# Stream work over sparse attention: value jobs of two head pairs opened a pair earlier, even shares, three score buffers

## The chip, the cores and the metric

The kernel runs on one core of a Trainium2 chip. A core has TensorE (PE; PEld is its weight load), VectorE (DVE), ScalarE (ACT), GpSimd (POOL) and SyncE (SP, which issues most DMAs). The metric is the device time of one execution in microseconds; the figure of a kernel is the median of its runs.

## What is computed

One layer of a streaming encoder for 1,024 prompt tokens and 32 sample tokens, in fp32: a modulated RMS norm, one input projection into ten parts, a state-space branch, a sparse attention branch, a gated merge and an output projection. The part that matters here is the attention. An indexer gives each query a score per key, the 256 best keys are kept, and the softmax runs over these alone:

```python
z = jnp.einsum('btd,de->bte', h, w_in)
u, zs, q, k, v, za, qi, ki, wi, gm = jnp.split(z, offs, axis=-1)
...
top_val, top_idx = lax.top_k(score, n_sel)
s = jnp.einsum('bthd,btkhd->bthk', q, kg) * (HEAD_DIM ** -0.5)
p = jax.nn.softmax(s, axis=-1)
o = jnp.einsum('bthk,btkhd->bthd', p, vg)
...
ya = o.reshape(B_, T, D_ATT) * jax.nn.silu(za)
merged = sigmoid(g_s) * (ys @ w_ps) + sigmoid(g_a) * (ya @ w_pa)
```

There are eight heads of 64; k and v of all tokens are outputs too.

## The kernel before

All products keep fp32 precision by splitting each operand into a high and a low part: three matmuls (wh x hH, wh x hL, wl x hH; lines 271 to 273) make one product of a 128-row block of weights with a block of tokens.

**The stream.** Projections are jobs of a stream `Z` (class Stream). A job K, V or Q makes 128 columns of k, v or q, those of one pair of heads, for three blocks of 256, 384 and 416 tokens: 24 steps of three matmuls into the PSUM tile pz. A job m makes 128 columns of `ys @ w_ps` in 12 steps. The jobs stand in the order K0 V0 Q0 (the first head pair), gates and za, then K1 V1 Q1 K2 V2 Q2 K3 V3 Q3 m0 to m7. Steps are emitted by `run(us)`: it adds to a credit and emits a step whenever the credit holds 0.483, so a credit unit is meant as a microsecond of matmuls. Only jobs up to the one named by `Z.upto` may run; `Z.until` runs the stream until a job is done. A job's weights are loaded (raw), cast (wh) and subtracted (wl) one to two jobs ahead, for K, V and Q on POOL (lines 263, 264), for m on ACT and POOL (259, 264).

**Jobs K and V** copy their result on ACT into a tile zf (lines 1318, 1323; two buffers). `tok_major` then transposes it on TensorE (line 1271) into token order, nine blocks in three parts, each copied by ACT into a tile tm (1273, 1279), which is stored to HBM as an output; tm has two buffers that K and V jobs share in turn. The tm of a V job is also the source of the value tiles: `values(e)` casts and subtracts it into V0 or V1 (1391, 1392). A small copy of the sample's rows, vts, has two buffers.

**The attention** is one sequence of items, 17 for each of the four head pairs (pairs 0 to 3 below): eight row blocks of 128 queries for head e=0, eight for e=1, and one for the sample tokens; the row block i has 128(i+1) keys. Pair 3 takes them in another order. An item is the chain score products on TensorE (line 1409, tile pss), masked minimum on VectorE (1415, into a score buffer Sm), exponential on ACT (1422), reciprocal and scaling (1427, 1429 or 1431), transposes on TensorE (1502, into the PSUM tile pt, two buffers), high and low part of the result (PH on ACT, 1504, PL on VectorE, 1505), value products on TensorE (1519, 1521, tile pspo) and their evacuation (1524, 1525, 1527). The loop emits it spread over four rounds: in round k stand the scores of item k, the scaling of k-1, the transposes of k-2 and the value products of k-3. Between them `run` is called three times, with 0.4, 0.3 and 0.3 of f:

```python
f = FA[p][e_] + FF * (it.i + 1 if it else 5)
```

FA is a number for each pair and head, FF is 0.08. So f is the stream work that an item gets. The order of TensorE, VectorE and ACT is the program's; POOL and SP are ordered by a scheduler.

**Limits on the stream.** At the beginning of pair 0 the jobs up to K2 are open, and in its middle the same; at pair 1 up to Q2, in its middle up to K3; at pair 2 up to Q3, in its middle up to m7. With two tm buffers, V2 cannot write its tm before pair 1's second value tile has been made from V1's, which happens three rounds into pair 1.

**Behind the attention** the remaining m jobs run, then the eight products with w_pa, each over four blocks of rows: block 3 is b3H/b3L, pair 3's result, split as it is made (line 75, 78); block 0 is loaded as y0 earlier; blocks 1 and 2 come back from HBM as src (1783) and are split (75, 78) into b. SP also loads the w_pa weights (250) and the first rows xo of the residual (1900) there.

Of the kernel before, what the change touches and what calls it, by code (L numbers as in the profile page):

```python
# [7 lines left out]
F32 = mybir.dt.float32  # L8
# [20 lines left out]
NS, NI = 6, 9  # L29
KF = 9.0  # L30
WB = 5
SQ, HF, SM, GD, GH, NP, BL, HB, GL = 1, 4, 4, (1, 1, 0), 1, (0, 0, 2, 2), 1, 1, 0
TP = 1000
PP = 2.0
W0, W1, W2, A1 = 4, 2, 4, 3
# [2 lines left out]
NP, HP = (0, 2), 100  # L38
# [2 lines left out]
KA, LA = 5.0, 1.0  # L41
RE = 2.9
LAG, RS, MS, RM, RB = 4.5, 4.6, 0.008, 14.0, 1
FA, FF, SA, SB = ((1.0, 0.95), (1.75, 1.75), (1.25, 1.25), (1.5, 1.5)), 0.08, 1.0, 2.5
YR = 3.9, 2.0, 2.0, 8.0, 3.0
MR, ML, YS, YW, HI, HG, JO, SF = (), 1, 10, 15, 0, 0, 8, (2, 2, 2, 1)
C_U, C_ZS, C_Q, C_K, C_V, C_ZA, C_QI, C_KI, C_GM = 0, 512, 1024, 1536, 2048, 2560, 3072, 3584, 3656
# [16 lines left out]
def body(nc, tc, I, O, dbg=None):  # L64
# [48 lines left out]
    def ps_t(n="pt"):  # L113
        t = psum.tile([128, 512], F32, tag="t", name=n)
        return t
# [459 lines left out]
    class Stream:  # L575
# [78 lines left out]
        def run(self, us):  # L654
            self.credit += us
            while self.credit >= self.STEP:
                us = self.step()
                if not us:
                    us = self.STEP
                    self.tick(us)  # L660
                self.credit -= us
# [18 lines left out]
    Z = Stream()  # L680
# [573 lines left out]
    ap_ = stT.enter_context(tc.tile_pool(name="at", bufs=1, side="right", reuse_waits="tile"))  # L1254
# [3 lines left out]
    vpo = O["v_p"].rearrange("a b (k p) h d -> p (a b k) (h d)", p=128)  # L1258
    kso = O["k_s"].rearrange("a b p h d -> (a b p) (h d)")
    vso = O["v_s"].rearrange("a b p h d -> (a b p) (h d)")  # L1260
    def cp(eng):
        return se.copy if eng is se else eng.tensor_copy

    def tok_major(src, outp, outs, name, fin_, eng):
        tm = ap_.tile([128, 9, 128], F32, name="tm", bufs=2)

        def part(b):
            pt = ps_t()
            for k in range(4 * b, min(9, 4 * b + 4)):
                n = 128 if k < 8 else 32  # L1270
                te.transpose(pt[:n, (k % 4) * 128:(k % 4) * 128 + 128], src[:, k * 128:k * 128 + n], idf)
            if b < 2:
                cp(eng)(tm[:, 4 * b:4 * b + 4].rearrange("p k c -> p (k c)"), pt)
                if wide[0]:
                    Z.after(TW, lambda: part(b + 1))
                else:
                    Z.banks.insert(0, lambda: part(b + 1))
            else:
                cp(eng)(tm[:32, 8], pt[:32, 0:128])
                sp.dma_start(outp, tm[:, 0:8])  # L1280
                sp.dma_start(outs, tm[:32, 8])
                fin_()
        Z.after(TF, lambda: part(0) if wide[0] else Z.banks.append(lambda: part(0)))
        return tm
# [23 lines left out]
    class Heads:  # L1308
# [43 lines left out]
        def kside(self):  # L1352
            self.kd = dram.tile([128, T], F32, name=f"kd{self.p}")
            sp.dma_start(self.kd, self.kf[:, 0:T])

            def fin_():
                ckt = ap_.tile([128, 4, 128], F32, name="ckt", tag="kd", bufs=2)
                kall = self.kall = ap_.tile([128, 544], F32, name="kall", bufs=2)
                sp.dma_start(ckt, ck[:, :, self.cs])
                se.copy(kall[:, 512:544], self.kf[:, T:NT])  # L1360

                def turn():
                    pt = ps_t()
                    for k in range(4):
                        te.transpose(pt[:, k * 128:(k + 1) * 128], ckt[:, k], idf)
                    se.copy(kall[:, 0:512], pt)
                    self.ready = True
                    self.heads()
                Z.after(TW if wide[0] else 2.5, turn if wide[0] else lambda: Z.banks.append(turn))
            tok_major(self.kf, kpo[:, :, self.cs], kso[:, self.cs], "k", fin_, self.eng)  # L1370

        def vside(self):
            def fin_():
                self.vts = ap_.tile([32, 128], F32, name="vts", bufs=2)
                ge.tensor_copy(self.vts, self.vt[:32, 8])
                Z.done.add(f"v{self.p}")
            self.vt = tok_major(self.vf, vpo[:, :, self.cs], vso[:, self.cs], "v", fin_, self.eng)

        def heads(self):
            if self.ready and self.want:  # L1380
# [224 lines left out]
    def m_load(f):  # L1605
        if f < 8:
            m1.append(late["fin"].tile([128, NT], F32, name="m1", tag=f"mm{f - 1}") if f else
                      stg.tile([128, NT], F32, name="m1", tag="stg"))
            sp.dma_start(m1[f], thD[f])
# [94 lines left out]
    at2 = stT.enter_context(tc.tile_pool(name="at2", bufs=1, side="right", reuse_waits="tile"))  # L1704
# [15 lines left out]
    for k in range(len(seq) + 3):  # L1720
        it = at(k)
        if k in first:
            p, begin = first[k]
            k0 = k
            if p:
                Z.until(f"Q{p}")
            if p == 3:
                b3H, b3L = (zfp.tile([128, NT], F32R, name=n, tag="zf", bufs=2) for n in ("b3H", "b3L"))
            else:
                Z.upto(f"Q{p + 1}" if p else "K2")  # L1730
            begin()
        if it:
            e_ = max(it.e, 0) if it.e >= 0 or p == 3 else 1
        f = FA[p][e_] + FF * (it.i + 1 if it else 5)
        if not k:
            run(RE)
        if it:
            it.scores()
        if k in half and p < 3:
            HD[p + 1].want.append(0)  # L1740
            HD[p + 1].heads()
            Z.upto(f"K{p + 2}" if p < 2 else "m7")
            if p == 2:
                m_load(0)
        if p and k == k0 + 2:
            HD[p].want.append(1)
            HD[p].heads()
        if it:
            it.maxima()
        if at(k - 1):  # L1750
            at(k - 1).norm(0)
        run(f * 0.4)
        Z.turns(2)
        if at(k - 3):
            at(k - 3).out()
        if k - 3 in end and end[k - 3][0] < 3:
            end[k - 3][1]()
            HD[p].values(1)
        if k + 3 in end and p < 3:
            Z.until(f"v{p + 1}")  # L1760
            HD[p + 1].values(0)
        run(f * 0.3)
        if at(k - 2):
            at(k - 2).turn()
        if at(k - 1):
            at(k - 1).norm(1)
        if it:
            it.exps()
        run(f * 0.3)
# [195 lines left out]
```

## Time and profile before

| | us |
|---|---|
| three runs | 1003.65, 1005.86, 1009.34 |
| median | 1005.86 |
| the profiled execution | 1004.61 |
| its span, first to last instruction | 1002.8 |
| attention, first score product to last value product | 589.85 to 844.6 |
| pairs 0, 1, 2, 3 in it | 50.4, 69.2, 63.3, 71.9 |

The profile gives, for one execution, when each instruction ran, on which engine and line, and what it waited for. A timeline row is start, duration, engine, line, operation, out<-in, shape and count, and in brackets the idle time of the engine before it with what ended it. A waits row is "engine, tile, line <- engine, tile, line: us in total, times, longest". Matmul rows overlap: their ends are modelled.

### The profile page before, as it was taken

To read this page: it belongs to the slowest core of one execution; us is meant where nothing else is said; L and a number is where in the kernel's file an instruction comes from. 1 tells how busy PE (TensorE), PEld (TensorE's weight loads), DVE (VectorE), ACT (ScalarE), POOL (GpSimd) and SP (SyncE) were. 2 spreads that over 40 slices of the span, in tenths; PEclk is the share of its full clock that TensorE was granted. 3 is DMA by queue.
4 is the path that set the end of the run, shared out by engine and by line. 5 is a ranking of instruction groups with operands and counts; after the bars stand their busy time and mean duration, and the time that the engine had idled before them with its cause. 6 is when DMAs were issued, how large, how long until landed. Compare 5 with 4: busy or idle time off the path is not lost. (4 is left out here: it accounts for less than half of the span.)

```text
span 1002.8 us, 16919 instructions
## 1 busy us (share of the span) xinstructions
PE 964.6 (96%) x6034; PEld 900.1 (90%) x6034; DVE 759.2 (76%) x1748; ACT 526.8 (53%) x1127; POOL 230.3 (23%) x435
## 2 busy tenths in 40 slices
PE   5999999999999999999999999999999999999997
PEld 2789999999899899999999988899898989998786
DVE  4659979994676868979998978767678786895543
ACT  3642234433655655867998356656576555443111
POOL 2202400000000012333323842433222222430000
PEclk9999999999999999999999999999999999999999
DMA  9923424436585220524213440231228503652311
GB/s 312 295 60 106 134 70 129 121 96 175 187 258 159 75 85 22 156 58 139 86 65 127 131 130 22 85 113 49 86 86 292 182 23 104 190 206 101 116 63 63
DMA packets 134255, 124.24 MB, mean 124 GB/s; under 512 B 20256, under 2 KB 114932, under 8 KB 134172
## 3 DMA queue, kind: packets, MB, share of 16 engines
q1 hardware_dynamic: 133232, 122.62, 39.7%
q8 instruction: 47, 0.77, 0.3%
q10 hardware_dynamic: 780, 0.52, 0.2%
q14 instruction: 36, 0.29, 0.1%
q0 software_dynamic: 160, 0.03, 0.0%
HBM read 87.74 MB, written 34.83 MB: 122 GB/s over the span
## 5 line engine op out<-in xcount | busy, mean ns | idle before, releaser
L271 PE MATMUL pz<-hH,wh 128*128 128x384 f32 (+4 forms) x760 | 258.2, 340 | 1.6 <-ACT zf L1323 1.6
L272 PE MATMUL pz<-hL,wh 128*128 128x384 f32 (+4 forms) x760 | 250.2, 329 | 0.0
L273 PE MATMUL pz<-hH,wl 128*128 128x384 f32 (+4 forms) x760 | 250.0, 329 | 0.0
L264 POOL TENSOR_TENSOR wl<-raw,wh 128x256 fp32r<-128x256 f32 (+1 forms) x176 | 125.8, 743 | 108.5 <-ACT wh L259 108.2
L271 PEld LDWEIGHTS pz<-hH,wh 128*128 128x128 f32 (+1 forms) x760 | 142.7, 188 | 6.5 <-ACT zf L1323 1.8
L272 PEld LDWEIGHTS pz<-hL,wh 128*128 128x128 f32 (+1 forms) x760 | 142.0, 187 | 2.0
L273 PEld LDWEIGHTS pz<-hH,wl 128*128 128x128 f32 (+1 forms) x760 | 141.7, 187 | 1.3
L1573 ACT ACTIVATE junkb<-sco,thr 128x768 bf16<-128x768 f32 (+3 forms) x128 | 96.7, 756 | 29.6 <-DVE thr L1655 19.1
L1575 DVE TENSOR_SCALAR_CACHE_REDUCE junk<-sco,thr 128x1024 bf16<-128x1024 f32 (+2 forms) x96 | 105.5, 1098 | 2.2
L271 PE MATMUL pss<-hH,wh 128*128 128x256 f32 (+2 forms) x288 | 92.7, 322 | 1.5 <-ACT tg L713 1.3
L272 PE MATMUL pss<-hL,wh 128*128 128x256 f32 (+2 forms) x288 | 90.8, 315 | 0.0
L273 PE MATMUL pss<-hH,wl 128*128 128x256 f32 (+2 forms) x288 | 90.5, 314 | 0.0
L263 POOL CAST wh<-raw 128x256 fp32r<-128x256 f32 x84 | 41.7, 536 | 175.4 <-PE pz L272 161.0
L1504 ACT CAST PH<-pt 128x512 fp32r<-128x512 f32 (+2 forms) x96 | 43.1, 482 | 35.3 <-PE pt L1502 30.9
L1505 DVE TENSOR_TENSOR PL<-pt,PH 128x512 fp32r<-128x512 f32 (+2 forms) x96 | 50.5, 553 | 14.0 <-ACT PH L1504 12.6
L1238 DVE SCALAR_TENSOR_TENSOR sco<-rl,wi,sco 128x384 f32<-128x384 f32 (+6 forms) x49 | 45.6, 939 | 18.3 <-ACT rl L1233 17.5
L271 PEld LDWEIGHTS pss<-hH,wh 128*128 128x128 f32 x288 | 55.6, 193 | 3.8 <-POOL wh L263 1.6
L1233 ACT ACTIVATE rl<-pss 128x384 f32<-128x384 f32 (+6 forms) x56 | 41.1, 738 | 28.5 <-PE pss L1231 21.3
L272 PEld LDWEIGHTS pss<-hL,wh 128*128 128x128 f32 x288 | 55.1, 191 | 0.3 <-DVE hL L78 0.2
L273 PEld LDWEIGHTS pss<-hH,wl 128*128 128x128 f32 x288 | 55.1, 191 | 0.0
L1422 ACT ACTIVATE Sm<-Sm,mx 128x128 f32<-128x128 f32 (+8 forms) x68 | 52.7, 774 | 2.6 <-DVE mx L1415 2.5
L1936 PE MATMUL psm<-o,mL 128*128 128x512 f32 (+1 forms) x136 | 52.0, 382 | 0.0
(409 smaller groups left out, 2171.9 us busy)
## 6 DMA issues: line engine op xcount, KB each, us to landing
raw<-in_w_in SPq DMA_DIRECT2D x44, 512.0 KB
thD<-tg SPq DMA_DIRECT2D x16, 528.0 KB
wm<-in_w_mod SPq DMA_DIRECT2D x8, 1024.0 KB
m<-thD SPq DMA_DIRECT2D x8, 528.0 KB
tgl<-thD SPq DMA_DIRECT2D x8, 528.0 KB
rraw<-in_w_mod SPq DMA_DIRECT2D x4, 1024.0 KB
kd<-kd SPq DMA_DIRECT2D x32, 128.0 KB
xo<-in_x_prompt SPq DMA_DIRECT2D x8, 512.0 KB
```

Of the source, the lines that this page charges most:

```text
L263: ge.tensor_copy(wh[:, c], raw[:, c])
L264: leng.tensor_sub(wl[:, c], raw[:, c], f32(wh[:, c]))
L271: te.matmul(ps, wh, xh, start=first, stop=False)
L272: te.matmul(ps, wh, xl, start=False, stop=False)
L273: te.matmul(ps, wl, xh, start=False, stop=last)
L1238: ve.scalar_tensor_tensor(sco[i][:m, :nk], rl[:m, :nk], w, sco[i][:m, :nk], op0=ALU.mult, op1=ALU.add)
L1422: se.activation(P, P, AF.Exp, scale=-1.0, bias=self.mx, accum_out=self.rs)
L1504: se.copy(PH[:, b0:b1_, oc], src)
L1505: ve.tensor_sub(PL[:, b0:b1_, oc], src, f32(PH[:, b0:b1_, oc]))
L1573: se.activation(junkb[:m, :nk], x[:m], AF.Sign, bias=t, accum_out=cnt[:m, k:k + 1])
L1575: ve.tensor_scalar(junk[:m, :nk], x[:m], t, None, op0=ALU.is_lt, op1=ALU.add, accum_out=cnt[:m, k:k + 1])
L1936: te.matmul(ps, ml, wh, start=False, stop=last)
```

## The change

Four edits. Every engine has the same instructions as before; only their order, and some buffers, differ.

```diff
-SQ, HF, SM, GD, GH, NP, BL, HB, GL = 1, 4, 4, (1, 1, 0), 1, (0, 0, 2, 2), 1, 1, 0
+SQ, HF, SM, GD, GH, NP, BL, HB, GL = 1, 4, 3, (1, 1, 0), 1, (0, 0, 2, 2), 1, 1, 0
...
-FA, FF, SA, SB = ((1.0, 0.95), (1.75, 1.75), (1.25, 1.25), (1.5, 1.5)), 0.08, 1.0, 2.5
+FA, FF, SA, SB = ((1.4, 1.3), (1.45, 1.45), (1.35, 1.35), (1.4, 1.4)), 0.08, 1.0, 2.5
...
     def tok_major(src, outp, outs, name, fin_, eng):
-        tm = ap_.tile([128, 9, 128], F32, name="tm", bufs=2)
+        tm = (at2 if name == "v2" else ap_).tile([128, 9, 128], F32, name="tm", bufs=2 - (name == "v2"))
...
-                self.vts = ap_.tile([32, 128], F32, name="vts", bufs=2)
+                self.vts = ap_.tile([32, 128], F32, name="vts", bufs=3)
...
-            self.vt = tok_major(self.vf, vpo[:, :, self.cs], vso[:, self.cs], "v", fin_, self.eng)
+            self.vt = tok_major(self.vf, vpo[:, :, self.cs], vso[:, self.cs], f"v{self.p}", fin_, self.eng)
...
-                Z.upto(f"Q{p + 1}" if p else "K2")
+                Z.upto(f"Q{p + 1}" if p else "V2")
...
-            Z.upto(f"K{p + 2}" if p < 2 else "m7")
+            Z.upto("m7" if p == 2 else f"V{p + 2}")
```

SM is the number of score buffers Sm. V2's tm gets a buffer of its own in the pool of the scores, so V3 follows K3 in the shared two. V2 may run in pair 0 and V3 in the second half of pair 1.

Counted by the score products that they follow, the stream steps of pairs 0, 1, 2, 3 and of the rest were 40, 72, 57, 62 and 25, and are 59, 64, 59, 59 and 15.

What moves is shown at two places. First TensorE at the end of pair 0, before: L1409 with kall is the sample item's score product, L1502 are transposes of scores, L1519 and L1521 value products, L1409 with qz the first of pair 1, L1271 the transposes of K2.

```order
L1502 MATMUL pt<-idf,Sm 128x128 x6
L1409 MATMUL pss<-kall,qsm 64x272 x2
L1519 MATMUL pspo<-PH,V_4837 128x256 x6
L1521 MATMUL pspo<-PL,V_4837 128x256 x6
L1502 MATMUL pt<-idf,Sm 128x128 x7
L1409 MATMUL pss<-kH_6687,qz 128x128
L1409 MATMUL pss<-kL_6688,qz 128x128
L271 MATMUL pz<-hH_84,wh 128x256
L272 MATMUL pz<-hL_85,wh 128x256
L273 MATMUL pz<-hH_84,wl 128x256
L1271 MATMUL pt<-idf,zf 128x128 x4
```

The same place on TensorE after the change, from the same six transposes on; the L271 to L273 are V2's.

```order
L1502 MATMUL pt<-idf,Sm 128x128 x6
L271 MATMUL pz<-hH_82,wh 128x384
L272 MATMUL pz<-hL_83,wh 128x384
L273 MATMUL pz<-hH_82,wl 128x384
L1409 MATMUL pss<-kall,qsm 64x272 x2
L271 MATMUL pz<-hH_738,wh 128x416
L272 MATMUL pz<-hL_739,wh 128x416
L273 MATMUL pz<-hH_738,wl 128x416
L1271 MATMUL pt<-idf,zf 32x128
L1519 MATMUL pspo<-PH,V_4837 128x256 x6
L1521 MATMUL pspo<-PL,V_4837 128x256 x6
L271 MATMUL pz<-hH_738,wh 128x416
```

Steps of V2 now stand between these products, and the last of K2's transposes has moved ahead of the value products.

Second SP's queue behind the attention, before: raw are the w_pa weights, xo the first residual rows, src and srs the results of pairs 1 and 2 that TensorE needs for w_pa.

```order
L250 DMA raw<-in_w_pa 128x4x128 x2
L1900 DMA xo<-in_x_prompt 128x1024 x2
L250 DMA raw<-in_w_pa 128x4x128
L1783 DMA src<-yaD_4279 128x1024
L1784 DMA srs_9787<-yaD_4279 128x32
L1783 DMA src<-yaD_4280 128x1024
L1784 DMA srs_9793<-yaD_4280 128x32
```

SP's queue at the same place after the change:

```order
L250 DMA raw<-in_w_pa 128x4x128 x3
L1900 DMA xo<-in_x_prompt 128x1024 x2
L1783 DMA src<-yaD_4279 128x1024
L1784 DMA srs_9818<-yaD_4279 128x32
L1783 DMA src<-yaD_4280 128x1024
L1784 DMA srs_9824<-yaD_4280 128x32
```

The third load of w_pa weights has moved from behind xo to ahead of it, so src follows xo directly. On TensorE, eight steps of m7 that stood between the products with b3 and those with block 0 stand ahead of b3 or within the attention now, and the two follow each other.

## The prediction

> **What bounds the kernel now.** I read the page first, then the timeline of TensorE where the attention begins, then busy time by stage, then who TensorE waited for.
>
> ```profile
> PE 964.6 (96%) x6034; PEld 900.1 (90%) x6034; DVE 759.2 (76%) x1748; ACT 526.8 (53%) x1127; POOL 230.3 (23%) x435
> ...
> PEclk9999999999999999999999999999999999999999
> ```
>
> TensorE is busy nearly throughout at full clock. But matmul rows overlap, so its real pace is the distance between starts:
>
> ```profile
> 593.82 0.34 PE L271 MATMUL pz<-hH,wh 128*128 128x384 f32 x1
> 593.99 0.34 PE L272 MATMUL pz<-hL,wh 128*128 128x384 f32 x1
> 594.16 0.34 PE L273 MATMUL pz<-hH,wl 128*128 128x384 f32 x1
> 595.98 0.30 PE L1502 MATMUL pt<-idf,Sm 128*128 128x128 f32 x1 [1.48 <-DVE Sm L1431]
> ```
>
> Rows last 0.34 but start 0.17 apart: a stream step of 384 columns (three matmuls) costs 0.52 us, and the mean step over the three blocks is 0.52 x 352/384 = 0.48. The last row is a stall: 595.98 - 594.16 - 0.17 = 1.65 us lost, of which the row shows 1.48. Such a wait is the only thing that the change can win, since it adds and removes no instruction. How many are there? The five windows are the four head pairs and the start of the w_pa products after them; the columns are start:end, length, then busy time (and instructions) of PE, PEld, DVE, ACT, POOL, then clock, DMA share and GB/s.
>
> ```profile
> 589.80:640.20 50.40, 46.65 (x306) 43.16 (x306) 38.41 (x120) 33.93 (x78) 16.58 (x38) 1.00 0.19 55
> 640.20:709.40 69.20, 67.02 (x461) 63.52 (x459) 46.70 (x137) 40.45 (x96) 22.93 (x46) 1.00 0.26 78
> 709.40:772.70 63.30, 60.35 (x416) 56.13 (x414) 46.93 (x137) 42.00 (x98) 18.41 (x38) 1.00 0.48 156
> 772.70:844.60 71.90, 70.70 (x482) 66.91 (x481) 54.68 (x155) 42.03 (x95) 17.86 (x43) 1.00 0.32 108
> 844.60:866.00 21.40, 20.70 (x129) 19.86 (x128) 13.62 (x26) 8.24 (x15) 8.83 (x18) 1.00 0.71 211
> ```
>
> Length less PE busy is idle time: 3.75, 2.18, 2.95 and 1.20 us by pair, 10.08 in all, and 0.70 after. Pair 0, with the least stream work, idles most. TensorE's waits in these pairs, one block of rows per pair:
>
> ```profile
> PE pspo L1521 <- DVE PL L1505: 1.5, 1, 1.5
> PE pt L1502 <- DVE Sm L1431: 1.5, 1, 1.5
> PE pt L1502 <- ACT Sm L1429: 0.5, 1, 0.5
> PE pss L1409 <- DVE mx L1415: 0.3, 1, 0.3
> ...
> PE pt L1271 <- DVE PL L1505: 1.3, 1, 1.3
> PE pt L1502 <- ACT tm L1279: 0.8, 1, 0.8
> ...
> PE pt L1502 <- DVE mx L1415: 0.9, 1, 0.9
> PE pt L1502 <- ACT tm L1273: 0.6, 1, 0.6
> ...
> PE pt L1502 <- ACT Sm L1429: 1.0, 2, 0.7
> ```
>
> Every one is the softmax chain of an item (minimum, exponential, scaling, transpose, split) not ready when TensorE arrives. Stream steps in front of it are what hides it. At most some 10 us (1%) can be had here.
>
> **The change part by part.** By the order of the two programs, the stream steps that stand in pairs 0 to 3 and behind them were 40, 72, 57, 62 and 25; now they are 59, 64, 59, 59 and 15. The sum, 256, is the same.
>
> *Pair 0: 19 steps more, 9.1 us of matmuls.* They are moved, not added; they count only for the idle time that they fill. In front of the 1.65 us stall above, 6 steps become 8: 2 x 0.52 = 1.0 us of it goes. In front of the stall on L1521 (item 8), items 6 to 8 get 1,088 columns more; at 0.52/384 a column that is 1.5 us, and it is about filled. The seam to pair 1:
>
> ```profile
> 639.55 0.93 PE L1502 MATMUL pt<-idf,Sm 128*128 128x128 f32 x7
> ...
> 640.77 0.28 PE L273 MATMUL pz<-hH,wl 128*128 128x256 f32 x1
> 642.39 0.66 PE L1271 MATMUL pt<-idf,zf 128*128 128x128 f32 x4 [1.35 <-DVE PL L1505]
> ```
>
> Here the stream had run dry (items 15 and 16 had one step between them, since only jobs up to K2 were open), and K2's transposes wait behind item 15's split for a PSUM tile. Now V2 is open and gives these two items seven steps; 642.39 - 640.77 - 0.12 = 1.5 us should mostly go. So pair 0 by its items: 1.0 + 1.5 + 1.5, with 0.5 of the small ones, 4.5 us.
>
> V2's other work moves into pair 0 with it:
>
> ```profile
> 607.53 1.62 POOL L263 CAST wh<-raw 128x256 fp32r<-128x256 f32 x4 [0.18 <-PE pz L272]
> 609.12 2.83 POOL L264 TENSOR_TENSOR wl<-raw,wh 128x256 fp32r<-128x256 f32 x4
> ...
> L1323 ACT COPY zf<-pz x10: 345/474/513, 426.5 to 739.6; 128x416 f32<-128x416 f32 x4, 128x256 f32<-128x256 f32 x3, 128x384 f32<-128x384 f32 x3
> ...
> L1273 ACT COPY tm<-pt x16: 558/586/593, 416.9 to 747.5; 128x512 f32<-128x512 f32 x16
> ```
>
> POOL splits its weights in 1.62 + 2.83 = 4.5 us (16.58 of 50.40 busy there: room). ACT copies 3 x 0.47 + 2 x 0.59 + 0.25 = 2.9 us, to 36.8 of some 55. VectorE gets nothing. SP gets V2's weight load and stores earlier; nothing of attention in pair 0 is queued behind them except K tiles needed half a pair later. I take zero for all these, but ACT's copies can stand ahead of an exponential: 0 to 0.8 us, the latter from the wait on tm above.
>
> *Pairs 1 to 3.* Pair 1 loses 8 steps (3.8 us of cover) and the seam's work. Items 24 to 26 lose 864 columns, 1.2 us of cover, but ACT's tm copies go from there too; the wait of 0.8 can grow to about that of pair 0 now (1.5). I take +0.3, bounds 0 to +1.5. Pair 2's boundary (items 33 to 35) gains 1,120 columns, 1.5 us: of the waits on tm there some 1 us goes. Elsewhere steps change by two or three: -0.3.
>
> *The sum over attention, from both sides.* By items it is -4.5 + 0.3 - 1.0 - 0.3 = -5.5. By stage it is smaller: charge the seam's 1.35 to the dry pair 0, and idle time against steps reads 5.10 at 40, 2.95 at 57, 1.20 at 62, 0.83 at 72. The pairs near 60 steps average 2.1; three pairs at 59 and one at 64 (1.1) give 7.4 against 10.08, -2.7. A straight line through the four points gives only -1.4, as even shares then merely move idle time. I take -3.3: nearest to the rows at 57 and 62 steps, as the new pairs look most like these, with a little of the item account.
>
> *Three score buffers.* The only place that a fourth would be missed is VectorE's minimum, which writes the new item's scores:
>
> ```profile
> L1415 DVE CUSTOM_DVE_ANT_0 Sm<-pss,mb 128x384 f32<-128x384 f32 (+6 forms) x68 | 35.8, 527 | 3.3 <-PE pss L1409 3.0
> ```
>
> It waits for the score products on TensorE, and in TensorE's order the transposes that free the buffer of three items earlier stand before these products. So zero. The Trainium skill (Perfetto Trace Analysis, Optimization Strategy) says that a gap repeating on the engine that should be saturated can mean too few buffers; by that, dropping one is the wrong way, which is a rival below. No wait of this trace names a score buffer. The separate V2 tile and the third vts issue nothing: zero.
>
> *The tail.* Ten steps (4.8 us) less stand behind the last item, where they covered the splits of the attention results:
>
> ```profile
> 844.35 0.41 PE L1521 MATMUL pspo<-PL,V 128*128 128x256 f32 x2
> 844.54 0.34 SPq L1900 DMA_DIRECT2D xo<-in_x_prompt  x1
> ...
> 846.10 0.62 ACT L75 CAST b3H<-qs 64x512 fp32r<-64x512 f32 x1 [0.31 <-DVE qs L1527]
> ...
> 848.24 0.46 PE L273 MATMUL psm<-b3H,wl 128*128 128x416 f32 x1 [0.53 <-POOL wl L264]
> 848.68 0.46 SPq L1783 DMA_DIRECT2D src<-yaD  x1
> ...
> 852.35 1.05 ACT L75 CAST b<-src 128x1024 fp32r<-128x1024 f32 x1 [4.43 <-DMA src<-yaD]
> 853.43 1.23 DVE L78 TENSOR_TENSOR b<-src,b 128x1024 fp32r<-128x1024 f32 x1 [1.46 <-ACT b L75]
> ```
>
> The load of src takes 852.35 - 848.68 = 3.67 us and ACT waits 4.43 for it, unseen, because eight m7 steps run meanwhile. Now three steps stand between the last value product (its stream ends at 844.6) and b3H: 846.3 on this clock, against 846.72, 0.4 lost. The wait on wl (0.53) goes, as those weights are split an item earlier. Twelve matmuls each on b3 and b0 (1.8 us) reach 850.4. In the new SP order src no longer stands behind the third w_pa load, so it issues right after xo, at about 845.0, and lands at 848.7 by the same 3.67. Its casts are done at 849.8 (high) and 851.0 (low, first needed at 851.0): just in time. I take +0.5, bounds 0 and the third rival.
>
> Sum: -3.3 + 0.5 = -2.8 us. The profiled execution took 1004.61 (span 1002.8), which gives 1001.8; the median of the three runs is 1005.86, 1.25 above it, which gives 1003.1. I say 1002.5.
>
> **The rivals.** (1) *The stalls really fill.* The item account, -5.5 + 0.5 = -5.0, and the small waits too: down to 1000.2, or 999 with another 1 us. For it: stalls are short against what is put before them. Against: the chain's VectorE work (38.41 of 50.40 in pair 0) is close behind, and a filled gap can shift to the next item. Chance 0.23. (2) *Idle time only moves*: the straight line, -1.4 + 0.5, about 1004.5; with pair 1's bound of +1.5, 1006. Chance 0.18. (3) *The tail starves.* The src loads follow 512 KB of xo on the same queue. If 1,024 KB drain at the span's mean of 124 GB/s instead of the 211 of the last window, the first src lands at 845.0 + 8.3 = 853.3, its cast at 854.4 against 850.4, and the second, 4.1 us later, costs about 2 more: 6 to 7 us of stall, -3.3 + 6.5 = +3.2, 1008.5 and slower than before. It decides from a landing later than 849.4; each us beyond is lost. For it: ACT already waits 4.43 there. Against: 211 GB/s in that window. The Trainium skill (DMA: Bandwidth & Descriptors, Queues, rings and completion order) has descriptors of one ring consumed in order, so src cannot overtake xo; no row here shows it. Chance 0.10. (4) *Three buffers bind*, the skill's rule: the score ring then behaves like the PSUM ring pt, whose waits on PL and tm in the rows above are 1.3 + 0.8 + 0.6 = 2.7, say 3 to 4: -2.8 + 3.5, about 1006. Chance 0.04, since the order puts the release first.
>
> **How the numbers follow.** My forecast has 0.45. Half a per cent (5 us) is about what a measurement of this kernel can tell from no change. Faster by more than that needs below 1000.8: rival 1 and a little of the forecast, 0.28. Slower needs above 1010.9: the worse half of rival 3 and little else, 0.06. The rest, 0.66, is the same. The range reaches from rival 1 with 1.5 us to spare, 998.7, to rival 3, 1008.8.
>
> **What would show it.** Idle time of TensorE by pair should be near 2 us in all four, with no wait of L1271 at the seam to pair 1 and the first stall near 0.6. Step by step wrong: pair 1 idle over 3 us; L1415 waiting for transposes or ACT; in the tail, PE at psm waiting for ACT b by more than 1 us. The whole is wrong if attention's matmul gaps still sum to 10 us, or if the tail gives back more than 3.

## The result, and the profile after

The changed kernel takes 997.31 us (median of 6 runs, 996.79 to 999.12), the kernel before 1005.18 on the same chip: ratio 0.9921, 95% interval 0.9908 to 0.9935. Two later comparisons on other occasions gave 0.9928 (0.9915 to 0.9941) and 0.9924 (0.9909 to 0.9939). It is faster by 0.7 to 0.8%, more than my likeliest case and more than the rival that had the stalls fill. The profiled execution took 997.35, its span is 995.6.

The page's line of busy times hardly moves:

```profile
PE 962.1 (97%) x6034; PEld 898.8 (90%) x6034; DVE 758.3 (76%) x1748; ACT 526.7 (53%) x1127; POOL 229.2 (23%) x435
```

The windows show more. These are the four head pairs of the changed kernel, each up to the next one's first score product, then the start of the w_pa products; columns as before.

```profile
588.06:644.30 56.24, 55.61 (x373) 52.60 (x372) 39.81 (x121) 36.61 (x86) 18.55 (x41) 1.00 0.26 73
644.30:707.22 62.92, 62.09 (x430) 59.14 (x429) 45.56 (x134) 39.71 (x94) 24.83 (x48) 1.00 0.24 77
707.22:769.42 62.20, 61.41 (x416) 57.37 (x415) 47.78 (x139) 40.63 (x96) 16.87 (x35) 1.00 0.62 197
769.42:840.11 70.69, 69.29 (x472) 65.06 (x471) 54.59 (x154) 41.93 (x95) 17.37 (x43) 1.00 0.19 64
840.11:861.50 21.39, 19.49 (x115) 17.96 (x114) 14.71 (x28) 8.61 (x16) 7.17 (x14) 1.00 0.75 242
```

Length less PE busy is 0.63, 0.83, 0.79 and 1.40 us: 3.65 in place of 10.08. In the last window it is 1.90 in place of 0.70. So attention won 6.4 us of idle time and the tail lost 1.2. The first stall is nearly gone (593.78 - 593.43 - 0.17 = 0.18 us where 1.65 were lost), and the four transposes of K2 that stood behind item 15's split start without a wait:

```profile
593.43 0.34 PE L273 MATMUL pz<-hH,wl 128*128 128x384 f32 x1
593.78 0.30 PE L1502 MATMUL pt<-idf,Sm 128*128 128x128 f32 x1
...
632.01 0.60 PE L1271 MATMUL pt<-idf,zf 128*128 128x128 f32 x4
636.96 0.60 PE L1271 MATMUL pt<-idf,zf 128*128 128x128 f32 x4
```

Of TensorE's waits in the pairs these are the longest that are left, one block of rows per pair:

```profile
PE pspo L1521 <- DVE PL L1505: 0.6, 1, 0.6
...
PE pt L1502 <- ACT Sm L1422: 0.8, 1, 0.8
...
PE pz L271 <- PE pz L273: 0.4, 1, 0.4
PE pt L1502 <- ACT tm L1273: 0.2, 1, 0.2
...
PE pt L1502 <- ACT Sm L1429: 1.2, 2, 0.7
```

In the tail, ScalarE and SyncE behind the last item of the changed kernel, and TensorE's waits there:

```profile
841.06 0.42 SPq L1783 DMA_DIRECT2D src<-yaD  x1
...
841.95 0.62 ACT L259 CAST wh<-raw 128x512 fp32r<-128x512 f32 x1 [1.15 <-PE pz L272]
842.59 0.61 ACT L75 CAST b3H<-qs 64x512 fp32r<-64x512 f32 x1
843.23 1.17 ACT L75 CAST b<-y 128x1024 fp32r<-128x1024 f32 x2
846.54 1.05 ACT L75 CAST b<-src 128x1024 fp32r<-128x1024 f32 x1 [2.14 <-DMA src<-yaD]
...
PE psm L271 <- ACT b3H L75: 1.2, 1, 1.2
PE psm L272 <- DVE b L78: 0.4, 1, 0.4
PE psm L271 <- ACT b L75: 0.2, 1, 0.2
```

For the experiments I use a finer measure, **lost time**: the distance between the starts of consecutive matmuls less what the first one's columns take back to back (0.175 us for 384 columns, 0.118 for 256, 0.190 for 416, 0.11 for 128, and the like for other widths), summed, with shorter distances as negative, over the matmuls from an item's first score product to the next item's. Items are numbered 0 to 67; item 17 is the first of pair 1, 34 of pair 2, 51 of pair 3, and item 67 runs on to the last matmul, so it holds the tail. The expectations below count attention up to its last value product, which adds about 1 us of item 67: their 18.9 and 11.7 are 17.9 and 10.7 here. In us:

| profile | 0-17 | 18-32 | 33-35 | 36-50 | 51-66 | 67 on |
|---|---|---|---|---|---|---|
| before | 7.53 | 1.69 | 2.34 | 3.80 | 2.50 | 2.58 |
| before, again (e10) | 7.53 | 1.69 | 2.32 | 3.81 | 2.48 | 3.17 |
| changed | 2.12 | 1.82 | 1.36 | 2.27 | 3.12 | 4.29 |
| changed, again (e6) | 2.14 | 1.83 | 1.38 | 3.11 | 3.00 | 4.33 |
| changed, third (e15) | 2.17 | 1.83 | 1.38 | 2.32 | 3.04 | 4.25 |
| three buffers only (e1) | 7.46 | 1.69 | 2.36 | 3.85 | 2.58 | 2.63 |
| openings, old shares (e2) | 6.32 | 0.78 | 1.28 | 8.48 | 2.51 | 3.91 |
| e2, keys on GpSimd (e16) | 6.31 | 0.84 | 1.29 | 3.82 | 2.50 | 4.05 |
| new shares only (e3) | 7.80 | 3.19 | 0.92 | 4.94 | 5.00 | 2.22 |
| thin pair 0 (e5) | 6.33 | 1.72 | 0.85 | 2.29 | 3.45 | 0.81 |

Profiles of one kernel agree within 0.12 us in nearly every group. The two that differ more are 36-50 in e6 (0.84 us, on matmuls that read b, which a load brings) and the tail of before (0.59, of which 0.4 is a second wait for GpSimd's split wl). By this measure attention gives 17.9 - 10.7 = 7.2 us, the tail takes 1.7. (One profiled execution, that of e9, took 4115 us; its trace is left out.)

### The profile page after: what moved, and what is told of

Same layout as the page of the kernel before. It is cut to its first block, busy times and chain, and to the rows that moved or that the text cites. A ratio compares the mean times of both kernels' runs of the same rounds, so it can differ in the third digit from the quotient of the medians.

```text
span 995.6 us, 16923 instructions
## 1 busy us (share of the span) xinstructions
PE 962.1 (97%) x6034; PEld 898.8 (90%) x6034; DVE 758.3 (76%) x1748; ACT 526.7 (53%) x1127; POOL 229.2 (23%) x435
## 4 chain that ended last, share of the span: by engine, by line
PE 54%; DVE 11%; ACT 10%; issue 4%; DMA 1%; POOL 1%; SPq 0%; POOLq 0%; ACTq 0%; DVEq 0%
PE pz L271 9%; PE pz L272 8%; PE pz L273 8%; ACT junkb L1573 7%; PE pss L1409 3%; PE pt L1502 3%; DVE junk L1575 3%; PE psm L1936 3%; PE psm L1934 3%; PE psm L1935 3%; PE pspo L1521 2%; PE pspo L1519 2%; PE pss L1230 2%; PE pss L1231 2%; PE psm L271 1%
## 5 line engine op out<-in xcount | busy, mean ns | idle before, releaser
L271 PE MATMUL pz<-hH,wh 128*128 128x384 f32 (+4 forms) x760 | 258.2, 340 | 0.8 <-ACT zf L1323 0.8
L273 PE MATMUL pz<-hH,wl 128*128 128x384 f32 (+4 forms) x760 | 249.8, 329 | 0.0
L271 PEld LDWEIGHTS pz<-hH,wh 128*128 128x128 f32 (+1 forms) x760 | 142.5, 188 | 5.9 <-issue 1.7
L273 PEld LDWEIGHTS pz<-hH,wl 128*128 128x128 f32 (+1 forms) x760 | 141.6, 186 | 1.3
L271 PE MATMUL pss<-hH,wh 128*128 128x256 f32 (+2 forms) x288 | 92.8, 322 | 1.5 <-ACT tg L713 1.4
L273 PE MATMUL pss<-hH,wl 128*128 128x256 f32 (+2 forms) x288 | 90.6, 315 | 0.0
L271 PEld LDWEIGHTS pss<-hH,wh 128*128 128x128 f32 x288 | 55.5, 193 | 3.8 <-POOL wh L263 1.6
L273 PEld LDWEIGHTS pss<-hH,wl 128*128 128x128 f32 x288 | 55.2, 192 | 0.0
```

Of the source, the lines that this page charges most:

```text
L271: te.matmul(ps, wh, xh, start=first, stop=False)
L273: te.matmul(ps, wl, xh, start=False, stop=last)
```

## The experiments

**Each part alone: e1, e2, e3.**

```diff
e1, from before:  -SQ, HF, SM, ... = 1, 4, 4, ...   +SQ, HF, SM, ... = 1, 4, 3, ...
e2, from changed: -FA = ((1.4, 1.3), (1.45, 1.45), (1.35, 1.35), (1.4, 1.4))
                  +FA = ((1.0, 0.95), (1.75, 1.75), (1.25, 1.25), (1.5, 1.5))
e3, from before:  the same line of FA, the other way round
```

> Before, with three score buffers in place of four and nothing else changed. My theory (the gain is stalls of TensorE in attention that the moved stream steps cover) expects nothing: 1005.2 us within 1 us, the first score product at 589.9, and TensorE's lost time in attention 18.9 us as before. The rival that the smaller score pool shifts something ahead of attention (the changed kernel reached its first score product 1.8 us earlier, in a stretch where the two programs are the same) expects 1003.4 and a first score product near 588.1. The rival that a fourth buffer is missed expects a loss, 1 us or more, with the minimum on VectorE (L1415) waiting for the transposes.

> The changed kernel with the old shares of stream work: value tiles opened a pair ahead and three score buffers, but the stream steps by pair are 46, 75, 55, 62 and 18 behind. My theory: items 0 to 14 have the same steps in front of them as before, so their stalls stay (5.2 us over items 2 to 9); the seam to pair 1 now has seven steps in front and loses its 1.7 us; items 33 to 35 have four steps more and lose 1.5 of their 2.3; the tail has seven steps less and gives back 1.0. Together -2.2: 1003.0 us. A rival, that the opening is the whole of it (the value tiles' work out of the crowded later pairs), expects 997.5. A second, that idle time follows the number of steps in a stage as I charged it in the prediction, expects -0.7.

> Before with the new shares and nothing else: four score buffers and the old openings, so that the stream runs dry in pair 0 after item 12 and items 12 to 16 have one step between them (40, 65, 60, 54 and 37 behind). My theory: items 2 to 9 lose their stalls as in the changed kernel (-4.7 us), and five dry items instead of two cost about 1.2 us each (two cost 2.35 before), +3.6; pairs 2 and 3 give -1. Together -2: 1003, bounds 1001 to 1005. If the shares were the whole of it, 998; if idle time follows the number of steps in a stage, pair 0 with its 40 steps keeps its idle time and the sum is 1005.

e1: 1005.64, ratio 1.0004 (0.9995 to 1.0014). The third buffer is free, as forecast. Its first score product came at 588.84. e2: 1007.49, 1.0024 (1.0013 to 1.0035), slower. e3: 1007.29, 1.0022 (1.0014 to 1.0031), slower too. So openings and shares cost 2.5 and 2.3 us alone, where I had expected each to win 2, and give 7.9 together. In e3 the dry end of pair 0 is as expected: items 13 to 17 lose 6.2 us (2.35 in items 16 and 17 before), while items 2 to 9 fall from 5.1 to 1.7. In e2 the seam loses only 0.5 instead of 1.7, and the items in front keep their stalls, as expected:

```profile
PE pt L1502 <- DVE Sm L1431: 1.5, 1, 1.5
PE pspo L1521 <- DVE PL L1505: 1.5, 1, 1.5
PE pt L1502 <- ACT Sm L1429: 0.5, 1, 0.5
PE pss L1409 <- DVE mx L1415: 0.3, 1, 0.3
```

What no theory of mine had is the 8.48 in items 36 to 50 of e2. SyncE, TensorE and TensorE's waits in e2 there; kd are loads of keys, b the right sides of the m products, to which the stream goes over after Q3:

```profile
752.94 1.08 SPq L1294 DMA_DIRECT2D kd<-kd  x2
754.07 0.58 SPq L1602 DMA_DIRECT2D b<-ysHD  x1
...
753.70 0.35 PE L273 MATMUL pz<-hH,wl 128*128 128x416 f32 x1
756.63 0.38 PE L271 MATMUL pz<-b,wh 128*128 128x256 f32 x1 [2.25 <-DMA b<-ysHD]
...
PE pz L271 <- DMA b<-ysHD: 2.3, 1, 2.3
PE pz L272 <- DMA b<-ysLD: 1.1, 2, 0.8
```

The loads of b were issued 0.4 us after Q3's last matmul had started, since SyncE stood at the key loads, which waited 8.4 us for a buffer that GpSimd's split (kL) frees. TensorE loses 4.7 us. In the changed kernel the same loads are issued 7.3 us ahead:

```profile
739.17 1.09 SPq L1294 DMA_DIRECT2D kd<-kd  x2
740.35 0.54 SPq L1602 DMA_DIRECT2D b<-ysHD  x1
...
747.63 0.35 PE L273 MATMUL pz<-hH,wl 128*128 128x416 f32 x1
747.82 0.28 PE L271 MATMUL pz<-b,wh 128*128 128x256 f32 x1
```

**Pair 0's old share in the changed kernel: e5.**

```diff
-FA = ((1.4, 1.3), ...
+FA = ((1.0, 0.95), ...
```

> The changed kernel with the old share in pair 0 alone: items 0 to 14 have the steps that they had before, and everything behind them has the new shares (46, 63, 60, 59 and 28 behind). My theory: the stalls at items 2 to 9 come back (4.7 us, less 1 us at item 4 that the changed kernel has new), so attention is 3.5 us better than before instead of 7.2; with 28 steps behind the last item the tail gives nothing back. 1001.7 us. The rival that the even shares and the opening in pairs 1 to 3 carry the gain expects 998; the rival that it is a step count by stage (46 instead of 59 in pair 0) expects 1000 at most a gain of 5 with no stall of its own in items 2 to 9.

998.51, 0.9934 (0.9921 to 0.9947). In pair 0 the waits are those of e2 above, to the tenth; with the rest of items 0 to 17, 4.2 us more are lost than in the changed kernel, where I had expected 3.7. The time is not 1001.7, because the tail, which I had at no change, gains: 28 steps stand behind the last item, TensorE waits for nothing there that the view shows, and 0.8 us are lost instead of 4.3. The cast of src is as late as ever; the steps cover it:

```profile
840.70 0.62 ACT L75 CAST b3H<-qs 64x512 fp32r<-64x512 f32 x1 [0.95 <-DVE qs L1527]
...
846.88 1.05 ACT L75 CAST b<-src 128x1024 fp32r<-128x1024 f32 x1 [3.75 <-DMA src<-yaD]
```

So the thick pair 0 of the change buys 4.2 us in pair 0 and gives 3.5 back in the tail, and most of the 7.9 is there without it.

**The changed kernel again: e6, and the tail: e7.**

```diff
e7:  -wh, wl = wparts(raw_a, 4, 128)
     +wh, wl = wparts(raw_a, 4, 128, heng=ge if f == 1 else None)
```

> The changed kernel once more, unaltered: beside the before kernel on the same chip, and for a second profile of the stretch ahead of attention. If the 1.8 us by which it reached its first score product earlier are spread between executions, that product comes anywhere from 588 to 590 us and TensorE's lost time in attention is 11.7 us again, item by item; if they belong to the kernel, 588.1 again. The ratio to before: 0.992.

> The changed kernel with one cast of the tail, that of the second w_pa product's weights, moved from ScalarE to GpSimd, so that ScalarE casts the last attention result (b3H) without waiting 1.15 us for a weight slot first. If ScalarE's order is what the tail lost: 1.2 us faster than the changed kernel, 996.1, with no wait on b3H beyond 0.2. If the landing of the source rows (src) is what binds behind it: the wait on b3H goes, but TensorE then waits as much longer for the casts of src (0.23 and 0.39 now), and the time is 997.3 less 0.3 at most.

e6: 998.34, 0.9928 (0.9915 to 0.9941); the first score product came at 589.08. e7: 998.75, 0.9942 (0.9928 to 0.9955), not faster. Its waits in the tail:

```profile
PE psm L271 <- DVE m L1815: 1.1, 1, 1.1
PE psm L271 <- ACT b L75: 0.6, 1, 0.6
PE psm L272 <- DVE b L78: 0.6, 2, 0.4
PE psm L271 <- ACT b3H L75: 0.3, 1, 0.3
```

The wait on b3H fell from 1.2 to 0.3, and what was won came back as longer waits on b and one on the merge (L1815) in the second product. ScalarE's order was the first of several waits, not the bound.

**The place of the switch, and fewer steps everywhere: e8, e9, e11.**

```diff
e8, from e2:         -(1.75, 1.75), (1.25, 1.25), ...   +(1.75, 1.75), (1.05, 1.25), ...
e9 and e11, changed: +FA = ((1.3, 1.2), (1.35, 1.35), (1.25, 1.25), (1.3, 1.3))
```

> Openings and buffers as in the changed kernel, shares as before except the first half of pair 2, 1.25 to 1.05: three or four steps fewer stand in front of the place where the stream goes over to its m products. With the share of 1.25 TensorE there lost 4.7 us, since the loads of their right sides (b, from the DRAM copy) were issued only when the last step of Q3 ended, behind the key loads on SyncE's queue. If that is the cost of that run (1007.5), the gap falls below 1 us and the time to 1002.5 to 1003.5, below before; the four steps behind attention give a few tenths more. If the openings themselves cost time, it stays at 1006 to 1007.5.

> The changed kernel with every share 0.1 lower: 56, 59, 56 and 51 steps by pair and 34 behind instead of 15. If the tail is short of steps (it lost 1.8 us against before with 15 and gained 1.8 with 28), the tail is 3.5 us better; if attention's stalls come back as the steps go from them, 1 to 3 us are given back there. Net 995 to 997, 995.5 the likeliest. If more steps in attention were worth their stalls one for one, 999.

> The changed kernel with every share 0.1 lower, once more for a profile that can be read (its time was 1001.4 us, 3 us above the changed kernel's on the same chip). If the stalls of attention came back one for one with the steps that left it, they show spread over many items, 3 to 5 us more than the 11.7 of the changed kernel, and a tail that loses under 0.5. If it is again the place where the stream goes over to its m products, one gap of 2 to 4 us stands there, with the loads of b issued less than 3 us ahead of it.

e8: 1004.91, 0.9998 (0.9986 to 1.0011), 2.6 us below e2 where I had expected 4 to 5: b is issued 1.3 us ahead, and 2.6 us are still lost on it. Its profiled execution took 1009.17, 4.3 us above its median, and loses 1.3 us less than e2's in attention but 1.5 more in the tail, so where the 2.6 us between the medians come from is not shown. e9: 1001.44, 0.9961 (0.9948 to 0.9975), 3 us above the changed kernel, where I had expected 2 us below. The profile of e11 (one execution, 1000.38) has 16.1 us of lost time in attention against 10.7, and a tail of 1.15 against 4.29. Both of my mechanisms are in it: of the 5.4 us more, 1.0 is at the switch (1.7 in place of 0.7, with b issued 2.4 us ahead), the rest spread over items 2, 8, 9, 18, 24, 42 to 44, 60 and 63, while items 4 and 26 lose 0.9 less each. My expectation had priced the return of stalls too low. It had also miscounted the steps: in the trace they are 56, 59, 56, 56 and 29, so 14 steps (6.8 us) out of attention, not 19, brought 5.4 us of stalls back.

**Before again, and the tail's other causes: e10, e12, e13.**

```diff
e12: -sp.dma_start(xts[i][:n], ...)   +(ge if i in (0, 2) else sp).dma_start(xts[i][:n], ...)
e13: as e12, and  +wh, wl = wparts(raw_a, 4, 128, heng=ve if f == 1 else None)
```

> The kernel before, unaltered, for a second profile of it. Item by item TensorE's lost time in attention should be as in the first profile (18.9 us); the first score product comes between 588 and 591 us if the stretch ahead of it varies from execution to execution, as the profiles of the other kernels suggest, and at 589.9 again if it doesn't.

> The changed kernel with the two xo loads that stand ahead of the src loads issued by GpSimd instead of SyncE. If src lands late because it is behind xo on one queue (5.5 us from issue to cast, against 3.7 in the kernel before, where xo had been issued 6.7 us earlier): it lands after about 3.7, its cast starts at some 844.5 instead of 846.5 on the changed kernel's clock, TensorE's two waits on b (0.40 and 0.56) go, and the time is 1 us shorter. If what src shares with xo is the engines' bandwidth and not the queue, the cast starts at 846 and nothing changes.

> The one before, and the cast of the second w_pa product's weights on VectorE instead of ScalarE, so that neither the weight slot nor the xo bytes stand in front of the tail's casts. If these two are what the tail lost, 2.0 to 2.3 us less than the changed kernel: 995 to 996. If src keeps its late landing, the wait on b3H goes and comes back as a wait on b, and the time is the changed kernel's within 0.5.

e10: 1004.19 (one execution), first score product at 588.87, lost time as in the table. e12: 998.14, 0.9938 (0.9918 to 0.9957): no gain that shows. ScalarE's casts of src in e12, and TensorE's waits there:

```profile
843.99 1.05 ACT L75 CAST b<-src 128x1024 fp32r<-128x1024 f32 x1
845.25 0.22 ACT L75 CAST b<-srs 128x32 fp32r<-128x32 f32 x1 [0.22 <-DMA srs<-yaD]
848.26 1.05 ACT L75 CAST b<-src 128x1024 fp32r<-128x1024 f32 x1 [2.79 <-DMA src<-yaD]
...
PE psm L271 <- ACT b3H L75: 1.2, 1, 1.2
PE psm L271 <- ACT b L75: 0.5, 1, 0.5
PE psm L272 <- DVE b L78: 0.4, 1, 0.4
```

Off xo's queue the first src is there 2.5 us earlier, the second no earlier than before (848.26 against 847.93). Each account has half of it: here the order within a queue decided which of the loads landed first, and what all four share, whichever queue they stand in, decided when the last one did. That agrees with the Trainium skill (DMA: Bandwidth & Descriptors, Queues, rings and completion order), by which a ring's descriptors are consumed in order while an engine alternates between the queues that have work for it. e13: 998.9, 0.9943 (0.9922 to 0.9964). The wait on b3H is 0.3, and GpSimd's split of the weights is now the late one. The issue of xo is not what holds it, as that ended 0.9 us before the split began; but its four parts take 4.23 us where they took 2.16 in e12, and the two longest (1.43 and 1.54) ran beside VectorE's subtractions of 128x1024 (L78, 1.30 and 1.21). Whether these slowed them is not shown.

```profile
842.65 4.23 POOL L264 TENSOR_TENSOR wl<-raw,wh 128x128 fp32r<-128x128 f32 x4 [0.92 <-PE pz L273]
...
PE psm L273 <- POOL wl L264: 2.4, 1, 2.4
PE psm L271 <- ACT b3H L75: 0.3, 1, 0.3
```

**Does a stall go by its item or by its pair: e14, e15.**

```diff
e14: -FA = ((1.4, 1.3), ...   +FA = ((1.4, 0.95), ...
```

> The changed kernel with the share of pair 0's second half back at 0.95, the first half kept at 1.4: items 0 to 8 have the same steps in front of them as in the changed kernel, items 9 to 16 five fewer in sum, and 22 steps stand behind the last item instead of 15 (53, 63, 60, 58 by pair). If a stall belongs to its item and to the steps just in front of it: pair 0 loses 2.1 us as in the changed kernel, though it has 6 steps fewer; pairs 1 to 3, which come out much as in the run with a thin pair 0, lose some 9; the tail loses about 2 instead of 4.3. The sum of 13 against 15.0 of the changed kernel gives 2 us less: 996. If idle time goes by a pair's number of steps, pair 0 loses 3 to 3.5 with 53 steps, and the time stays within 0.5 of the changed kernel's.

> The changed kernel, unaltered, beside the one before it in this list on the same chip. Attention loses 10.7 to 11.5 us and the tail 4.3 as in its first two profiles; 997 to 998.5.

e15: 997.30, as expected. e14: 1002.79, 0.9976 (0.9964 to 0.9988), where I had expected 996. Items 0 to 8 lose 1.2 us in both kernels, so these stalls do go by the steps in front of them. But items 9 and 14 lose 0.55 and 0.64 more: the steps taken from there (six, by the count of the pairs) were not spare, and pair 0 as a whole (3.4) came out where the account by pairs had put it. The larger part is elsewhere: b was issued 0.5 us ahead of Q3's last matmul and cost 3.3 us, item 42 lost 1.2 more, and the tail lost 3.9, as src landed 6 us after its issue.

**The switch by itself: e16, e17.**

```diff
-                sp.dma_start(kd[64 * hf_:64 * hf_ + 64], X.kd[64 * e:64 * e + 64, c])
+                (ge if X.p == 3 else sp).dma_start(kd[64 * hf_:64 * hf_ + 64], X.kd[64 * e:64 * e + 64, c])
```

> The run with the openings and the old shares (1007.5 us), with the key loads of the last head pair (L1294) issued by GpSimd instead of SyncE, so that the loads of b, the right sides of the m products, are no longer queued behind key loads that wait for GpSimd's split. If TensorE's 4.7 us at the place where the stream goes over to the m products come from that queue: b is issued some 5 us or more ahead of the last step of Q3 instead of 0.4 behind it, the waits on b fall below 1 us, and the time to 1003.0 to 1003.8, which is also what my account by items had given for that run without this gap. If they come from the load itself or from the memory that b takes over, 1007.5 as before.

> The changed kernel with the same move of the key loads, as a control: there b was issued 7.3 us ahead and TensorE lost 0.7 on it. By the queue account nothing is left to win: the changed kernel's 997.3 to 998.3, within 1 us, plus what the issue costs on GpSimd. If the move itself wins or costs more than 1 us here, the run above has to be read with that in mind.

e16: 1001.47, 0.9972 (0.9961 to 0.9983), against 1007.49 without the edit and 1003.0 to 1003.8 expected. e17, the control: 998.14, 0.9942 (0.9924 to 0.9961), no change from the 997.3 to 998.3 of the changed kernel. SyncE, GpSimd and TensorE in e16:

```profile
745.07 0.38 SPq L1602 DMA_DIRECT2D b<-ysHD  x1
...
753.73 1.05 POOL L1294 DMA_DIRECT2D kd<-kd  x2 [0.29 <-POOL kL L78]
...
754.20 0.35 PE L273 MATMUL pz<-hH,wl 128*128 128x416 f32 x1
754.64 0.36 PE L271 MATMUL pz<-b,wh 128*128 128x256 f32 x1
```

The key loads come as late as in e2, but b is no longer behind them: it is issued 9.1 us ahead, and nothing is lost on it. All other items of e16 lose what they lost in e2, save item 48 (1.3 against 0.3). The queue is the cause. Over all kernels the lost time on the matmuls that read b goes by that lead:

| issue of b ahead of Q3's last matmul, us | lost on matmuls that read b, us |
|---|---|
| -0.4 (e2) | 4.7 |
| 0.5 (e14), 0.6 (e3) | 3.3, 2.9 |
| 1.3 (e8) | 2.6 |
| 2.4 (e11) | 1.7 |
| 6.3 (e5), 6.9 (before), 7.3 (changed), 8.5 (e17), 9.1 (e16) | 0.6, 0.0, 0.7, 0.7, 0.0 |

The 0.6 and 0.7 of the last row are most likely not for b. They are one wait at the second block of m0, for which the profile names no DMA, and TensorE goes on 0.10 us (0.11 in e5 and e17) after VectorE has copied the last of Q3's result out of its PSUM tile pz. In the changed kernel:

```profile
750.35 0.19 DVE L1343 COPY qsm<-pz 64x32 f32<-64x32 f32 x1
750.64 0.41 PE L271 MATMUL pz<-b,wh 128*128 128x384 f32 x1 [0.44 <-PE pz L273]
```

No version came out faster than the changed kernel. Four score buffers beside V2's own tile were not run, so whether the change needs the room that the third one makes is not shown.

## Why the prediction was wrong

Forecast 1002.5 with 998.7 to 1008.8; the kernel takes 997.3 to 998.3. The step that failed is the sum over attention, "I take -3.3". I had a sum by items (-5.5) and cut it towards an account by pairs (-2.7). Measured, as lost time, it is -7.2. That is 3.9 us of the 5.2 by which the forecast missed; the tail, mis-sized too, took 1.2 back. Of the 2.5 that are neither, 0.4 to 0.8 are a shorter wait ahead of attention, for which I had no term, and the rest is open (last point).

- *By items*, my terms against the runs: pair 0 with the seam, items 0 to 17, -4.5, measured -5.4. Pair 1 +0.3, measured +0.1 (items 18 to 32). Pair 2's boundary -1.0, measured -1.0. The rest -0.3, measured -0.9. Together -5.5, measured -7.2. A stall's own size and the columns put before it were the right units, and a sound sum would have stood at -5.5. Not every wait that I listed was the softmax chain, though: the two on tm (0.8 and 0.6) were ACT's copies of the stream's own transposes.
- *By pairs*, I read idle time against steps in four pairs and gave a pair of 59 steps 2.1 us. Four pairs of 59 to 64 steps idle 0.63, 0.83, 0.79 and 1.40. The old figures belonged to where the steps stood, not to their number: e14 and e11 have pairs of 53 to 60 steps with a lost time from 2.4 to 7.9.
- *That a filled gap shifts to the next item* was my argument against rival 1. New stalls came at three items, 4, 46 and 58 (0.96, 1.1 and 0.4 us), against some 10 us filled. Rival 1, with 0.23, was the nearest case, and its 999 still too high.
- *The tail*, +0.5 forecast, +1.7 measured. I had src land 3.67 us after its issue and called it just in time; it took 5.5, behind two xo loads of 512 KB, not one as I wrote. And the cast of the second weights, which ScalarE has ahead of b3H, waited 1.15 for a slot that m7's last steps hold. That wait was in the order and I priced only SyncE's move. Rival 3's mechanism is there, but TensorE lost only 0.96 us in its two waits on b, a seventh of the 6.5 of its price, and e12 shows nothing won by taking xo off the queue.
- *Three buffers at nothing*: right, 1.0004. The rule on repeating gaps (Trainium skill, Perfetto Trace Analysis, Optimization Strategy) does not apply here: no gap came with the buffer's loss.
- *SP's queue in attention* I called harmless, "nothing of attention in pair 0 is queued behind them". In pair 0 that held. I never asked what stood queued where the stream changes over, and there the two halves of the change decide: either alone loses 3 to 5 us on b at that place, both together most likely nothing.
- *The sum.* Lost time gives -7.2 + 1.7 = -5.5, and from the first score product to the end the profiles agree (413.0 and 413.5 before, 407.5, 408.3 and 407.5 after). From the median before, 1005.2, that alone leads to 999.7, which is inside the range. Part of what went below it lies ahead of attention. TensorE's order is the same there in all programs, but one wait is shorter after the change; the first row is before, the second after:

```profile
576.42 0.44 PE L271 MATMUL pz<-hH,wh 128*128 128x384 f32 x1 [1.64 <-ACT zf L1323]
574.59 0.44 PE L271 MATMUL pz<-hH,wh 128*128 128x384 f32 x1 [0.81 <-ACT zf L1323]
```

The copy zf stands on ACT behind a count (L1663) that waits for VectorE's selection of the keys (le, L1662). TensorE waits 1.6 to 1.7 us in all profiles without the new openings (before, e10, e1, e3), and 0.8, or 1.2 in e2, e6 and e7, in all with them. So the change has a part of 0.4 to 0.8 us there, and three buffers alone (e1) have none; why the selection comes earlier is not shown. Most of the other difference ahead arises in the first 43 us and is as large between two executions of one kernel (1.3 us between before and e10). The medians differ by 6.8 to 8.3, of which 5.9 to 6.3 are accounted for; the remaining 0.5 to 2.4 us are open.

## What to carry to other kernels

Price a stall by its own rows: its length, and the work that the new order puts right before it; do not discount that by an average over a stage. When a knob moves work in time, look for every place where the bound engine goes over to data that a load brings, and read the lead of that load's issue over the first use, with what its queue waits for: in this kernel that margin cost nothing down to some 6 us, and from 2.4 on down about a microsecond for each one lost. Work taken from in front of a tail is paid for there, and removing one late step of a tail that has three only names the next.

## What was unexpected of the hardware

Lost time of a matmul order repeats to some 0.02 us per item in most items from execution to execution (7.53 and 7.53 over 18 items), while the first 43 us of the same two executions differ by 1.3 us. Two loads of 512 KB behind two others, on one queue or on two, were all in place some 8 us after the first issue (840.19 to 847.93 in the changed kernel, 840.12 to 848.26 in e12): 2 MB in 8 us, an estimate of about 260 GB/s that leaves out other loads of the same time.
